# Memory scores moved to the next pair's second turn, and two multiplications of the output norm given out later

## The chip, the cores and the metric

The kernel runs on one core of one Trainium2 chip. Its metric is the time of one execution in microseconds (us), as the device measures it. Below, TensorE (PE in the profile) does the matmuls and the transposes, VectorE (DVE) and ScalarE (ACT) the elementwise work and the reductions, GpSimd (POOL) masks and some products, and SyncE (SP) issues most of the DMAs. PEld in the profile is the loading of a matmul's stationary operand.

## The reference

One layer of a hybrid decoder over 4096 prompt tokens, with a small batch of 64 sampled tokens beside it, all in float32 with a model width of 1024:

```python
h = _rmsnorm(x, g_pre)
z = h @ w_in                       # one projection for all three groups
...
out_a = jax.nn.silu(cg) * cb * conv              # gated short convolution, 256 channels
o_b = _window_prompt(q, k, v, sink_g)            # window of 128, 8 heads of 64, sinks
out_b = jax.nn.silu(ag) * o_b
o_c = _mem_attend(mq, mem_k, mem_v)              # 4 heads into 256 memory tokens
out_c = jax.nn.silu(mg) * o_c
y = jnp.concatenate([out_a, out_b, out_c], axis=-1) @ w_out
return x + _rmsnorm(y, g_post), ...
```

Two pieces matter here. The memory attention's softmax is `exp(s - max)` over 256 keys, divided by its sum. And the output norm is `y * rsqrt(mean(y * y) + eps) * g_post`, added to `x`.

## The kernel before

**Stages.** The input projection fills the first part of the span: its last matmuls of line 368 end at 935.9 us. Then attention and output projection run together. The 4096 tokens are 16 chunks of 256, and each chunk has two halves of 128 queries, numbered h (chunk h // 2, half h % 2). The output projection takes the first six blocks of 128 tokens plainly (class `Block`, lines 1579 to 1661), and the other 26 blocks as 13 pairs (class `Pair`, line 1663 on), c = 3 to 15. A pair multiplies two blocks with both column halves of `w_out` by a scheme of sums and differences that needs fewer products. Each operand is split into a rounded high part and a low part (`lows`, line 1675: an ACT cast, then a DVE subtraction), and three matmuls (high by high, low by high, high by low) make one step of 128 in depth.

**Turns.** `Pair.run` (line 1730) issues 30 such steps, called turns here, of three matmuls of 128x512 each. In order: turns 0 and 1 (T3) and 2 and 3 (T4) start the accumulators c12 and c21; 4 and 5, then 6 and 7, add the row sums `pr`; 8 to 11 add `pw0` into c12; 12 and 13 add `pw1` into c21; 14 and 15 start c11 with the diagonal sum `pd`; 16 and 17 end c21; 18 and 19 add the differences `pc`; 20 to 23 end c11; 24 and 25 start c22; 26 to 29 end it. Before the matmuls of a turn, the functions registered for it are called, in the order of registration.

**Attention by turns.** Three functions serve a half h. `first_half(h)` (line 1885) transposes the memory probabilities of half h-1 (`xt`, line 1366), multiplies the window scores of h (`ws`, line 1331), multiplies both probabilities of h-1 with the values (lines 1388, 1394, 1059) and issues the window softmax. `memory_half(h)` (line 1906) multiplies the memory scores of h (`xs`, line 1353), and issues their maxima (`xmx`, line 1169), the negatives of these (`xnm`, line 1170), the exponentials (line 1178, ACT), the reciprocals of the sums (line 1184, DVE) and the factors on the probabilities (line 1190, POOL). `second_half(h)` (line 1912) transposes the window probabilities (`wt`, line 1376), copies them (line 1305, ACT), masks them on POOL in two selections each (`wpv`, line 1310, and `wpt`, line 1313), and loads keys and queries of half h+2. In a pair c from 3 on, half 2c+3 has them at turns 12, 16 and 19, and half 2c+4 at turns 24, 27 and 32; turn 32 is turn 2 of the next pair. Below, halves 2c+3 are the odd ones and 2c+4 the even ones.

**Order.** In pairs 3 to 12 TensorE runs in the order in which the program is written (`manual_schedule`). On the other engines a planner places each instruction when the kernel is compiled: of those that it takes to be ready by its own costs, the one written first. `keep_in_program_order(ins)` adds one edge: `ins` comes behind the instruction written just before it on its engine. On the chip each engine then follows its own order.

**Buffers.** The scores `xs`, the transposes `xt` and the products `wo` share one place of two PSUM banks. Four accumulators a pair share two more banks in turn. A high and low part takes one of four slots left in the pool of the weights. The queries have two slots, so those of half h+2 wait for the readers of half h.

**Ends of a pair.** A finished quarter is copied or added into `y`, squared on ACT with a sum (`square`, line 1748), and multiplied by the norm's weights `gpost` on DVE (line 1760 in `squared`, line 1770 in `scaled`, which for the first block of a pair is on POOL). `Block.finish` (line 1655) scales the row and adds `x` (line 1658).

Of the kernel before, what the change touches and what calls it, by code (L numbers as in the profile page):

```python
# [8 lines left out]
F32 = mybir.dt.float32  # L9
# [3 lines left out]
ALU = mybir.AluOpType  # L13
AX = mybir.AxisListType

P = 128
# [11 lines left out]
NCH = 4096 // CT  # L28
EPS = 1e-6
SCALE = 0.125  # L30
# [22 lines left out]
def hybrid_layer(ctx: ExitStack, tc: tile.TileContext, a: dict):  # L53
    nc = tc.nc
    TE, V, S, G, DMA = nc.tensor, nc.vector, nc.scalar, nc.gpsimd, nc.sync
# [14 lines left out]
    diag = const.tile([P, 2 * HW], F32, name="mix_s")  # L70
# [835 lines left out]
    last = NBLK - 1  # L906
# [161 lines left out]
    class Chunk:  # L1068
# [94 lines left out]

            return *(self.cross_unit(2 * j + hh, pts[hh]) for hh in range(2)), both

        def cross_maximum(self, h, s):
            c, nb = self.c, CT // P
            mx, nm = (tiny.tile([P, 4], F32, tag=n, name=f"x{n}{c}_{h}") for n in ("mx", "nm"))
            V.tensor_reduce(mx[:, :nb], s, axis=AX.X, op=ALU.max)
            V.tensor_scalar(nm[:, :nb], mx[:, :nb], -SCALE, None, op0=ALU.mult)  # L1170
            return nm

        def cross_exps(self, h, s, nm, p=None):
# [173 lines left out]
        def memory_scores(self, i):  # L1347
            c = self.c
            x = two_banks("x", f"xs{c}_{i}").rearrange("p a (h k) -> p a h k", h=2)
            for h in range(4):  # L1350
                q = self.q[i][:, h]
                for part in range(2):
                    TE.matmul(x[:, h // 2, h % 2], q, third["mk"][:, part, h, :], start=part == 0, stop=part == 1)  # L1353
            nms = [self.cross_maximum(2 * i + j, x[:, j]) for j in range(2)]
            self.xp = work([P, 2, 2, CT], "p", f"xp{c}_{i}")
            self.xps = [self.cross_exps(2 * i + j, x[:, j], nms[j], self.xp[:, j]) for j in range(2)]
            for j in range(2):
                self.cross_shares(2 * i + j, self.xps[j])
# [304 lines left out]
    class Pair:  # L1663
# [50 lines left out]

        def diagonal_sum(self):
            self.diagonal = self.parts("pd")[:, :, 0:2]
            self.sums_of(sums["sum"].tile([P, 512], F32, tag="sum", name=f"diag{self.c}"), self.diagonal, (self.mix(slice(2, 4), 0), self.mix(slice(0, 2), 1), ALU.add))()

        def column_differences(self):
            t = self.parts("pc")  # L1720
# [9 lines left out]
        def run(self, starts, sample=lambda: None):  # L1730
            c, last = self.c, self.c == NCH - 1
            t, at = third["wt"], [0]
            b11, b22 = [wo[2 + k][0] for k in range(2)], [wo[k][1] for k in range(2)]
            y = self.y = [work([P, D], "yn", f"yn{c}_{n}") for n in range(2)]
# [13 lines left out]
            def square(n, p, src, junk, pinned=False):  # L1748
                x = S.activation(junk, src, AF.Square, scale=float(D) ** -0.5, accum_out=st[n][:, p : p + 1])
                if pinned:  # L1750
                    tc.keep_in_program_order(x)
# [3 lines left out]
                S.copy(y[n][:, cs], acc)  # L1755

            def squared(n, p):
                cs = (left_, right_)[p]
                square(n, p, y[n][:, cs], s4, True)
                V.tensor_tensor(y[n][:, cs], y[n][:, cs], gpost[:, cs], op=ALU.mult)  # L1760

            def added(n, p, acc):
# [33 lines left out]
            done(1, 0, c21)  # L1796
            product(c11, self.down[1], t["T7"], False)
            squared(1, 0)
            product(c11, self.w[0], plain(0, range(4, 8)), False)
            added(0, 0, c11)  # L1800
            if not last:
                c22 = psum("z", f"y{c}_c22")
                between.append(lambda: (scaled(0, 0, True), ends(0)))
                product(c22, self.down[0], t["T6"], True)
                product(c22, self.w[1], plain(1, range(4, 8)), False)
                added(1, 1, c22)
                while behind:
                    behind.pop(0)()
                scaled(1, 1)
                ends(1)  # L1810
                return
# [59 lines left out]
    PLAIN_PAIRS = 3  # L1871
# [58 lines left out]

    first_at = {2: 4, 3: 20, 4: 34, 5: 48, 6: 62, 7: 76, 8: 89}
    turn_of = lambda odd, even: {h: start_of((h - 3) // 2) + (odd if h % 2 else even) for h in range(9, 2 * NCH + 1)}
    memory_at = {h: n + (7 if h == 2 else 3 if h == 8 else 3) for h, n in first_at.items()} | turn_of(16, 27)
    second_at = {h: n + (12 if h == 2 else 9 if h == 8 else 8) for h, n in first_at.items()} | turn_of(19, 32)
    first_at |= turn_of(12, 24)

# [3 lines left out]
    def at(n, fn):  # L1940
        what.setdefault(n, []).append(fn)
# [17 lines left out]
    for c, p in pairs.items():  # L1959
        e = start_of(c)  # L1960
        at(e - 10, p.plain_parts)
        at(e - 3, p.row_sums)
        if c == NCH - 2:
            at(e + 27, lambda: left.pop(0)(True))
        at(e + 4, lambda p=p: p.window_parts(0))
        at(e + 5, lambda: pending.pop()() if pending else None)
        at(e + 6, lambda: left.pop(0)(True) if left else None)
        at(e + (5 if c == NCH - 1 else 7), lambda p=p: p.window_parts(1))
        at(e + (7 if c == NCH - 1 else 9), p.diagonal_sum)
        at(e + (8 if c == NCH - 1 else 11), p.column_differences)  # L1970
        at(e + (9 if c == NCH - 1 else 11), lambda p=p: p.differences(True) if p.c == NCH - 1 else between.append(lambda: p.differences(True)))
        at(start_of(c - 1) + 6, p.load)
        if c == NCH - 1:
            at(e + 4, finish_block)
# [146 lines left out]
```

## Time and profile before

| what | value |
|---|---|
| three executions | 1522.27, 1523.91 and 1524.03 us; median 1523.91 |
| the profiled execution | 1528.73 us, of which the span from first to last instruction is 1527.0 us |
| busy, of the span | PE 99%, PEld 91%, DVE 79%, ACT 55%, POOL 26% |
| granted TensorE clock, mean | 0.998 |
| starts of pairs 3, 4 and 5 | 1049.87, 1086.51 and 1121.98 us |
| start of pair 15, and the end | 1476.55 and 1527.0 us |

A row of the timeline has the start, the time from the first to the last of the merged instructions, the engine, the line, the operation, what is written and read, the shape and the count; in brackets stands the idle time of the engine before it and what ended that. The profile counts a matmul as busy to its modelled end, which lies beyond the start of the next one, so a short wait of TensorE can lie inside its busy time. What a wait costs is read from the starts: a turn of three matmuls begins 0.69 us after the one before it when nothing holds it.

### The profile page before, as it was taken

How to read it: one execution, taken by the hardware profiler on the slowest of the kernel's cores; microseconds unless marked ns; L12 is line 12 of the kernel's file. 1: busy time of each engine (PE TensorE's matmuls, PEld its weight loads, DVE VectorE, ACT ScalarE, POOL GpSimd, SP SyncE). 2: the span in 40 equal slices, each digit the busy share in tenths (PEclk: the TensorE clock that was granted, in tenths of full speed). 3: DMA queues.
4: the chain of work that ended last, by engine and by line, in shares of the span. 5: the costliest groups of instructions: out<-in, count | busy, mean ns of one | idle time of the engine just before them, and what ended most of it. 6: DMA issues, size and time to landing. Idle time of an engine off the chain costs nothing.

```text
span 1527.0 us, 30947 instructions
## 1 busy us (share of the span) xinstructions
PE 1507.6 (99%) x11497; PEld 1384.4 (91%) x11497; DVE 1199.3 (79%) x2089; ACT 843.5 (55%) x2066; POOL 398.5 (26%) x576
## 2 busy tenths in 40 slices
PE   9999999999999999999999999999999999999997
PEld 8999999999999999999999999777888788888875
DVE  5779887899988777897677768777877788878874
ACT  5776665566322222354455536666666666666652
POOL 0223322211400000000111311234445544455641
PEclk9999999999999999999999999999999999999999
DMA  9989999978855333478687698988765555666552
GB/s 258 168 250 221 289 290 259 265 243 303 209 183 182 118 121 126 161 235 295 222 261 232 213 305 254 282 241 235 201 169 160 156 164 161 175 171 170 153 196 75
DMA packets 217322, 319.71 MB, mean 209 GB/s; under 512 B 37397, under 2 KB 143381, under 8 KB 217141
## 3 DMA queue, kind: packets, MB, share of 16 engines
q1 hardware_dynamic: 196837, 273.54, 60.8%
q0 software_dynamic: 19616, 43.15, 10.5%
q8 instruction: 91, 1.49, 0.4%
q10 hardware_dynamic: 720, 1.05, 0.2%
q14 instruction: 58, 0.48, 0.1%
HBM read 208.50 MB, written 110.15 MB: 209 GB/s over the span
## 4 chain that ended last, share of the span: by engine, by line
PE 75%; DMA 11%; DVE 6%; issue 4%; POOL 2%; ACT 1%; SPq 1%; DVEq 0%; ACTq 0%; POOLq 0%
PE c L368 39%; PE y_c L1746 16%; PE y L1637 3%; PE ws L1331 3%; DMA nat<-in_x_p 2%; DMA md<-th 2%; PE wo L1394 2%; PE wo L1059 2%; PE xs L1353 2%; PE xt L1366 2%; PE wt L1376 2%; PE wo L1388 2%; DMA place<-in_xt 1%; DMA wr_3A<-in_w_in 1%; DMA hd_B<-place 1%
## 5 line engine op out<-in xcount | busy, mean ns | idle before, releaser
L375 DVE TENSOR_TENSOR z<-c,z 128x520 f32<-128x520 f32 (+1 forms) x308 | 194.6, 645 | 83.5 <-PE c L368 82.5
L1746 PE MATMUL y_c<-wo,pw 128*128 128x512 f32 (+1 forms) x636 | 158.9, 392 | 0.6 <-DVE yn L1784 0.6
L1287 ACT ACTIVATE sm<-sm,wnm 128x128 f32<-128x128 f32 x256 | 99.4, 389 | 72.0 <-DVE wnm L1281 72.0
L1746 PEld LDWEIGHTS y_c<-wo,pw 128*128 128x128 f32 x636 | 114.0, 188 | 27.8 <-issue 5.4
L1190 POOL TENSOR_SCALAR xp<-xp,xrd 128x256 f32<-128x256 f32 x128 | 71.8, 577 | 196.9 <-DVE xrd L1184 192.3
L1178 ACT ACTIVATE xp<-xs,xnm 128x256 f32<-128x256 f32 x128 | 59.0, 473 | 38.3 <-DVE xnm L1170 22.9
L737 POOL CAST wmask<-negs 128x256 uint8<-128x256 f32 x1 | 1.1, 1149 | 266.6 <-DMA negs<-in_wmask 266.6
L1637 PE MATMUL y<-wo,mh 128*128 128x512 f32 x192 | 64.5, 398 | 0.2 <-ACT y L1646 0.2
L1310 POOL TENSOR_SCALAR_AFFINE_SELECT wpv<-wpt 128x512 f32<-128x512 f32 x62 | 56.9, 939 | 8.7 <-ACT wpt L1305 8.4
L1313 POOL TENSOR_SCALAR_AFFINE_SELECT wpt<-wpt 128x512 f32<-128x512 f32 x64 | 46.3, 742 | 38.6 <-ACT wpt L1305 38.2
L1331 PE MATMUL ws<-kst,q 128*128 128x256 f32 (+1 forms) x480 | 55.7, 297 | 0.0
L1341 DVE COPY_PREDICATED sm<-wmask,ws 128x512 f32<-128x512 uint8 x60 | 40.5, 729 | 19.0 <-ACT sm L1340 19.0
L276 ACT ACTIVATE nat<-nat 104x1024 f32<-104x1024 f32 x40 | 42.3, 1058 | 23.6 <-DMA nat<-in_x_p 23.5
L1658 DVE SCALAR_TENSOR_TENSOR xr<-yn,yst,xr 128x1024 f32<-128x1024 f32 (+2 forms) x35 | 51.3, 1470 | 2.9 <-POOL yst L1653 2.8
L407 ACT CAST zh<-z 128x520 fp32r<-128x520 f32 x56 | 33.3, 624 | 34.6 <-DVE z L375 31.9
L377 ACT COPY z<-c 128x520 f32<-128x520 f32 (+1 forms) x44 | 24.4, 554 | 50.5 <-PE c L368 47.2
L1331 PEld LDWEIGHTS ws<-kst,q 128*128 128x128 f32 (+1 forms) x480 | 46.4, 187 | 4.1
L1287 ACT ACTIVATION_READ_ACCUMULATOR sm<-sm,wnm 128x1 f32 x256 | 47.9, 187 | 0.0
L1295 DVE TENSOR_TENSOR sm<-sm,wrd 128x512 f32<-128x512 f32 x64 | 44.5, 696 | 1.1
L1746 PE MATMUL y_c<-wo,pc 128*128 128x512 f32 (+1 forms) x162 | 45.2, 400 | 0.0
L164 POOL DMA_DIRECT2D md<-th x48 | 26.3, 549 | 71.3 <-DVE th L425 61.0
L1637 PEld LDWEIGHTS y<-wo,mh 128*128 128x128 f32 x192 | 36.1, 188 | 8.9 <-issue 1.0
(1037 smaller groups left out, 5556.9 us busy)
## 6 DMA issues: line engine op xcount, KB each, us to landing
q<-qd SPq DMA_DIRECT2D x168, 128.0 KB
xr<-in_x_p SPq DMA_DIRECT2D x32, 512.0 KB
nat<-in_x_p SPq DMA_DIRECT2D x39, 416.0 KB
o_yp<-xr SPq DMA_DIRECT2D x31, 512.0 KB
kst<-qd SPq DMA_DIRECT2D x112, 128.0 KB
md<-th POOLq DMA_DIRECT2D x48, 260.0 KB, 7.2
qd<-zh SPq DMA_DIRECT2D x48, 260.0 KB
qd<-z SPq DMA_DIRECT2D x48, 260.0 KB
```

Source lines behind the costliest of these rows:

```text
L368: TE.matmul(bank[:, :HW], l, r, start=first and i == 0, stop=last and i == 3 * KH - 1)
L375: add = lambda dst, other: V.tensor_tensor(dst, c, other, op=ALU.add)
L1178: S.activation(p[:, i, :], s[:, i, :], AF.Exp, bias=nm[:, i : i + 1], scale=SCALE, accum_out=den[:, i : i + 1])
L1190: G.tensor_scalar(p[:, i, :], p[:, i, :], self.rds[h][:, i : i + 1], 0.5, op0=ALU.mult, op1=ALU.mult)
L1287: S.activation(sm[:, hh, :], sm[:, hh, :], AF.Exp, bias=nm[:, hh : hh + 1], scale=SCALE, accum_out=den[:, hh : hh + 1])
L1295: V.tensor_tensor(sm, sm, rd.unsqueeze(2).to_broadcast([P, 4, P]), op=ALU.mult)
L1310: G.affine_select(pv.rearrange("p (h q) -> p h q", h=4), p3, pattern=[[0, 4], [-1, P]], compare_op=ALU.is_gt, fill=0.0, base=0, channel_mu ...
L1313: G.affine_select(p3, p3, pattern=[[0, 4], [1, P]], compare_op=ALU.is_ge, fill=0.0, base=0, channel_multiplier=-1)
L1331: TE.matmul(out(kvh, col, bank), q(kvh, col, bank)[r], k(kvh, part)[r], start=first, stop=True, skip_group_check=not first, **place)
L1637: TE.matmul(acc, self.hl[l][:, k], wo[k][p][:, r], start=k + i == 0, stop=k + i == KT + 1)
L1658: x = V.scalar_tensor_tensor(self.xr[:m, cs], yn[:m, cs], st[:m, 3:4], self.xr[:m, cs], op0=ALU.mult, op1=ALU.add)
L1746: TE.matmul(acc, a[:, l, k], w[:, r, cs], start=first, stop=k == len(ws) - 1 and i == 2, skip_group_check=not new)
```

## The change

Four things are moved or bound.

- `cross_maximum` can bind the negative behind the instruction written before it on DVE, and `memory_scores` asks for that.
- The memory scores of the even halves are issued at turn 32 in place of turn 27, so at turn 2 of the next pair, behind the transposes and loads of `second_half` of the same half. That holds for halves 10 to 30, eleven in all.
- The parts of the window's outputs, `pw0` and `pw1`, are issued at turns 1 and 2 in place of 4 and 7 (4 and 5 in the last pair). Both of their instructions stay bound behind what is written before them on ACT and DVE.
- In `squared` the multiplication by `gpost` becomes a function of its own, `gained`. That of the first block's right half, written after turn 13 so far, is written after turn 19; that of the second block's left half, after turn 19 so far, is written after turn 25 (in the last pair directly behind the other). In the first pair the low part of the diagonal sum is bound behind what is written before it on DVE.

No instruction is added or taken out.

```diff
-        def cross_maximum(self, h, s):
+        def cross_maximum(self, h, s, pinned=False):
             c, nb = self.c, CT // P
             mx, nm = (tiny.tile([P, 4], F32, tag=n, name=f"x{n}{c}_{h}") for n in ("mx", "nm"))
             V.tensor_reduce(mx[:, :nb], s, axis=AX.X, op=ALU.max)
-            V.tensor_scalar(nm[:, :nb], mx[:, :nb], -SCALE, None, op0=ALU.mult)
+            negated = V.tensor_scalar(nm[:, :nb], mx[:, :nb], -SCALE, None, op0=ALU.mult)
+            if pinned:
+                tc.keep_in_program_order(negated)
             return nm
...
-            nms = [self.cross_maximum(2 * i + j, x[:, j]) for j in range(2)]
+            nms = [self.cross_maximum(2 * i + j, x[:, j], True) for j in range(2)]
...
         def diagonal_sum(self):
             self.diagonal = self.parts("pd")[:, :, 0:2]
-            self.sums_of(sums["sum"].tile([P, 512], F32, tag="sum", name=f"diag{self.c}"), self.diagonal, (self.mix(slice(2, 4), 0), self.mix(slice(0, 2), 1), ALU.add))()
+            x = self.sums_of(sums["sum"].tile([P, 512], F32, tag="sum", name=f"diag{self.c}"), self.diagonal, (self.mix(slice(2, 4), 0), self.mix(slice(0, 2), 1), ALU.add))()
+            if self.c == PLAIN_PAIRS:
+                tc.keep_in_program_order(x)
...
             def squared(n, p):
+                square(n, p, y[n][:, (left_, right_)[p]], s4, True)
+
+            def gained(n, p):
                 cs = (left_, right_)[p]
-                square(n, p, y[n][:, cs], s4, True)
                 V.tensor_tensor(y[n][:, cs], y[n][:, cs], gpost[:, cs], op=ALU.mult)
...
             product(c11, self.down[1], t["T7"], False)
             squared(1, 0)
+            gained(0, 1)
+            if last:
+                gained(1, 0)
             product(c11, self.w[0], plain(0, range(4, 8)), False)
             added(0, 0, c11)
             if not last:
                 c22 = psum("z", f"y{c}_c22")
                 between.append(lambda: (scaled(0, 0, True), ends(0)))
                 product(c22, self.down[0], t["T6"], True)
+                gained(1, 0)
                 product(c22, self.w[1], plain(1, range(4, 8)), False)
...
-    memory_at = {h: n + (7 if h == 2 else 3 if h == 8 else 3) for h, n in first_at.items()} | turn_of(16, 27)
+    memory_at = {h: n + (7 if h == 2 else 3 if h == 8 else 3) for h, n in first_at.items()} | turn_of(16, 32)
...
-        at(e + 4, lambda p=p: p.window_parts(0))
+        at(e + 1, lambda p=p: p.window_parts(0))
         at(e + 5, lambda: pending.pop()() if pending else None)
         at(e + 6, lambda: left.pop(0)(True) if left else None)
-        at(e + (5 if c == NCH - 1 else 7), lambda p=p: p.window_parts(1))
+        at(e + 2, lambda p=p: p.window_parts(1))
```

## The prediction

> **What bounds the kernel now.** I read the page's engine table first, then the windows of the third and of an ordinary pair, then the table of waits over the pair stage, then the timeline of each engine around the waits that stood out.
>
> ```profile
> PE 1507.6 (99%) x11497; PEld 1384.4 (91%) x11497; DVE 1199.3 (79%) x2089; ACT 843.5 (55%) x2066; POOL 398.5 (26%) x576
> ```
>
> TensorE bounds the whole span, and no work of it is removed. So the change can only take away or add moments in which TensorE stands still. The next view is the windows of pair 3 (1049.87 to 1086.51) and of a later pair: columns are the stretch, its length, then PE, PEld, DVE, ACT, POOL and SP busy, and the granted clock last but two.
>
> ```profile
> 1049.87:1086.51 36.64, 35.89 (x237) 28.80 (x236) 26.68 (x63) 23.96 (x82) 15.63 (x23) 1.00 0.82 207
> 1192.95:1228.45 35.50, 35.50 (x237) 28.69 (x236) 28.48 (x65) 24.02 (x82) 17.43 (x23) 1.00 0.60 168
> ```
>
> The clock is 1.00 in both. The later pair shows PE busy throughout, but this is by modelled ends; the loads fill only 28.69 of 35.50. The table of waits of the loads, over 1049 to 1527 (total us, times, longest), finds what lies hidden; its largest row that this change touches:
>
> ```profile
> PEld wo L1388 <- POOL wpt L1313: 4.1, 11, 0.4
> ```
>
> Eleven times, once a pair, the products with the window probabilities (line 1388) wait for POOL's last selection. In the timeline (start, length, engine, line, operation, what is written and read, shape, count), first at turn 12 and then at turn 24:
>
> ```profile
> 1204.94 0.43 PE L1388 MATMUL wo<-wpv,vt 64*64 64x256 f32 x2
> ...
> 1205.54 0.65 PE L1394 MATMUL wo<-wpv,vt 128*64 128x256 f32 x4
> ```
>
> ```profile
> 1220.21 0.43 PE L1388 MATMUL wo<-wpv,vt 64*64 64x256 f32 x2
> ...
> 1221.36 0.65 PE L1394 MATMUL wo<-wpv,vt 128*64 128x256 f32 x4
> ```
>
> At turn 12 the group of line 1388 takes 0.60 (1204.94 to 1205.54); at turn 24 it takes 1.15 (1220.21 to 1221.36): 0.55 lost. The chain behind it, on DVE, ACT and POOL:
>
> ```profile
> 1212.05 0.66 DVE L1169 TENSOR_REDUCE xmx<-xs 128x2 f32<-128x512 f32 x1
> 1212.63 0.68 DVE L1295 TENSOR_TENSOR sm<-sm,wrd 128x512 f32<-128x512 f32 x1
> 1213.23 0.69 DVE L1760 TENSOR_TENSOR yn<-yn,gpost 128x512 f32<-128x512 f32 x1
> 1213.83 0.16 DVE L1170 TENSOR_SCALAR xnm<-xmx 128x2 f32<-128x2 f32 x1
> 1213.90 0.68 DVE L1169 TENSOR_REDUCE xmx<-xs 128x2 f32<-128x512 f32 x1
> ```
>
> ```profile
> 1214.68 0.47 ACT L1178 ACTIVATE xp<-xs,xnm 128x256 f32<-128x256 f32 x1 [1.25 <-DVE xmx L1169]
> ```
>
> ```profile
> 1216.08 1.85 POOL L1190 TENSOR_SCALAR xp<-xp,xrd 128x256 f32<-128x256 f32 x4 [5.83 <-DVE xrd L1184]
> 1217.88 1.68 POOL L1310 TENSOR_SCALAR_AFFINE_SELECT wpv<-wpt 128x512 f32<-128x512 f32 x2
> 1219.51 1.22 POOL L1313 TENSOR_SCALAR_AFFINE_SELECT wpt<-wpt 128x512 f32<-128x512 f32 x2
> ```
>
> POOL works without a gap from 1216.08 to 1220.73. It was idle for 5.83 before, until a reciprocal. That came from exponentials, for which ACT had stood idle 1.25 until the second maximum ended at 1214.58. And DVE put a multiplication by `gpost` (line 1760, 0.60 from start to start) between the first maximum and its negative.
>
> **The change part by part.**
>
> *Multiplications given out later (odd halves).* Line 1760 is now written after turn 19, behind the maxima of turn 16. The second maximum and all that follows start 0.60 earlier. The loss is only 0.55, so it would be gone,. But ready by then, line 1760 can still slip in between the second maximum and its negative; the first exponentials then start as early, the second 0.60 later than they could, and POOL has two of its four factors to do meanwhile (0.93, half of 1.85), so I lose 0.1 of it. The gain lies between 0.4 and 0.55; I take 0.45. Eleven pairs: 11 x 0.45 = 4.95 less, at most 6.05. The multiplication itself moves into slack: its result is read only by `finish` in the next pair. In the last pair nothing moves but one multiplication, beside idle time; nothing.
>
> *Pins on the negatives.* Each reads the maximum written just before it. The edge holds an order that data holds already: the row at 1213.83 comes behind 1212.05 in any case, and nothing forbids the planner to put others between. Zero, from both sides, for the waits; what the planner then orders differently is in the range.
>
> *The third pair.* Here the low part of `pw0` and of the diagonal go ahead of what TensorE needs:
>
> ```profile
> 1054.42 0.69 DVE L1781 TENSOR_TENSOR s<-s,y_c 128x512 f32<-128x512 f32 x1 [1.57 <-PE y_c L1746]
> 1055.03 1.07 DVE L1679 TENSOR_TENSOR pw<-mix,pw 128x512 fp32r<-128x512 f32 x1
> 1056.02 0.85 DVE L1679 TENSOR_TENSOR pd<-diag,pd 128x256 fp32r<-128x256 f32 x1
> 1056.80 0.67 DVE L1784 TENSOR_TENSOR yn<-s,y_c 128x512 f32<-128x512 f32 x1
> ```
>
> ```profile
> 1054.15 2.88 PE L1746 MATMUL y_c<-wo,pr 128*128 128x512 f32 x12
> 1057.61 3.00 PE L1746 MATMUL y_c<-wo,pw 128*128 128x512 f32 x12 [0.58 <-DVE yn L1784]
> ```
>
> The same two groups of TensorE in the later pair:
>
> ```profile
> 1196.80 2.96 PE L1746 MATMUL y_c<-wo,pr 128*128 128x512 f32 x12
> 1199.59 2.94 PE L1746 MATMUL y_c<-wo,pw 128*128 128x512 f32 x12
> ```
>
> From the row sums to `pw0` it takes 3.46 in pair 3 and 2.79 in the later pair, so 0.67 is lost. With `pw0` at turn 1 its low part falls into DVE's idle 1.57 ahead of 1054.42, and the diagonal goes behind what it is written after. Gain 0 to 0.67; I take 0.6. This happens once.
>
> *Memory scores at turn 32 (even halves).* The eight matmuls of `xs` leave turn 27 and come at turn 2 of the next pair. TensorE's work is the same; DVE's and POOL's queue changes. DVE, in the order of the later pair, and the load of TensorE that waits for it:
>
> ```profile
> 1196.13 0.21 DVE L1652 TENSOR_SCALAR yst<-yst 128x1 f32<-128x1 f32 x1 [0.45 <-ACT s L1749]
> 1196.26 1.17 DVE L1770 TENSOR_TENSOR yn<-yn,gpost 128x512 f32<-128x512 f32 x1
> 1197.36 0.68 DVE L1781 TENSOR_TENSOR s<-s,y_c 128x512 f32<-128x512 f32 x1
> 1198.10 0.70 DVE L1679 TENSOR_TENSOR pw<-mix,pw 128x512 fp32r<-128x512 f32 x1
> ```
>
> ```profile
> 1198.09 1.23 PEld L1746 LDWEIGHTS y_c<-wo,pr 128*128 128x128 f32 x6 [0.18 <-DVE s L1781]
> ```
>
> The sum of line 1781 ends at 1198.04 and TensorE's second half of the row sums, which reads it, is loaded from 1198.09, after 0.18 of waiting: no slack. Before it now come the two maxima. When can they start? The moved `xs` stand behind these transposes, and as their time has left turn 27, they end about where the transposes end now, near 1195.4:
>
> ```profile
> 1194.32 1.03 PE L1376 MATMUL wt<-ident,sm 128*128 128x128 f32 x8
> ```
>
> From there DVE has the maxima (0.58 each, 1212.05 to the next start), the tiny row (0.13 to the next start), line 1770 and perhaps the low part of `pw0` (0.61 to the next start, an estimate from the 0.60 of its kind above). With line 1770 at 0.60 the sum starts at 1197.3 without the low part, 1197.9 with it, against 1197.36 now: 0 to 0.55 late. With line 1770 at the 1.17 that it takes today it would be 1.0 late at the worst. Its cost hangs on what POOL does beside it:
>
> ```profile
> L1770 DVE TENSOR_TENSOR yn<-yn,gpost x12: 682/1168/1174, 1089.8 to 1478.4; 128x512 f32<-128x512 f32 x12
> ```
>
> The columns are least, median and most in ns: 0.68 occurs. POOL's factors of the memory, beside it today, move behind this place, so I count with 0.68. I take the low part ahead of the sum in one pair of four, 0.15 a pair, 11 x 0.15 = 1.65 more, and keep 0 to 0.6 (6.6).
>
> `pw1` goes to turn 2 with its cast and low part bound behind what is written before them; it is due only at turn 12. Loads of queries for half h+2 wait for the later `xs`, and SP's other loads behind them, but the next reader comes 22 turns later, some 15 us. Both cost nothing, unless a queue is held; the bound is the second rival's.
>
> POOL of the even half (the factors, then behind them the selections and a difference), and the transposes on TensorE that read the factors:
>
> ```profile
> 1196.86 1.38 POOL L1190 TENSOR_SCALAR xp<-xp,xrd 128x256 f32<-128x256 f32 x2
> ```
>
> ```profile
> 1199.18 2.21 POOL L1310 TENSOR_SCALAR_AFFINE_SELECT wpv<-wpt 128x512 f32<-128x512 f32 x2
> 1201.34 1.67 POOL L1313 TENSOR_SCALAR_AFFINE_SELECT wpt<-wpt 128x512 f32<-128x512 f32 x2
> 1202.98 1.46 POOL L1693 TENSOR_TENSOR yn<-mix 128x512 f32<-128x512 f32 x1
> ```
>
> ```profile
> 1202.37 1.03 PE L1366 MATMUL xt<-ident,xp 128*128 128x128 f32 x8
> ```
>
> Selections (3.88 together) now go ahead of the factors (2 x 1.38 = 2.76). TensorE needs the factors at turn 12, from 1202.37, the last of them half of the group later, so about 1202.8, or 1202.3 with TensorE 0.45 earlier. The 6.6 of work can begin when the transposes `wt` are done, at 1195.4, and end at 1202.0; if the difference of 1.46 goes ahead of the last factors, at 1203.5. I take 1202.3, no wait, and keep 0 to 1.2 a pair for the range.
>
> Sum: -4.95 - 0.6 + 1.65 = -3.9. The profiled execution (1528.73, span 1527.0) becomes 1524.8; it stands 4.8 above the median of 1523.91, so for the median: 1520.0. A change under 0.2% (3.05 us) can't be told from none here.
>
> **A rule of the skill against the trace.** Line 1760, by its line:
>
> ```profile
> L1760 DVE TENSOR_TENSOR yn<-yn,gpost x26: 683/756/1074, 1071.2 to 1499.3; 128x512 f32<-128x512 f32 x26
> ```
>
> The rows of line 1770 (0.68 at least, 1.17 mostly) and of line 1760 (0.68 to 1.07) show that these multiplications take longer at some places than at others; the place at 1196.26 has POOL's factors beside it. The Trainium skill, page "SBUF — State Buffer", section "Who interferes with whom", says that a DVE instruction with two SBUF inputs contends with a GpSimd instruction that reads SBUF, and that the loser stands still for all of the other; the trace agrees at line 1770. By that rule the multiplication, moved to turn 19 and later, would take time from POOL's chain between 1216 and 1220.7: by the rule the sum is 1525.0, the third rival's; without it, 1520.0.
>
> **The rivals.**
>
> 1. *The even half's DVE queue gives the gain back.* For it speaks that line 1781 has no slack now; against it, the 0.49 by which line 1770 should be shorter. The low part of `pw0` goes ahead of the sum in every pair, 0.55 a pair in place of 0.15: 11 x 0.4 = 4.4 more than forecast, 1524.4, no change.
>
> 2. *POOL's factors come too late for turn 12 (the other side).* For it: 3.88 of selections now go ahead of them, and a difference of 1.46 may. Against: POOL had 5.83 of idle in the odd half, and its queue isn't full. It decides from an end of the factors after 1202.3 on; at 1203.2 TensorE waits 0.9 a pair, 11 x 0.9 = 9.9 more than my sum has, and 1.65 goes out since line 1781 has then no wait behind an earlier one: 1520.0 + 9.9 - 1.65 = 1528.3. At an end of 1202.5 it is 0.2 a pair and the kernel is as fast as forecast.
>
> 3. *The moved multiplication slows POOL.* The two factors at 1196.86, beside line 1770, take 1.38, where half of the four at 1216.08 take 0.93: 0.45 lost. In the odd chain that takes the whole 0.45 back: 1520.0 + 4.95 = 1525.0, and some of it is saved where line 1760 falls in a selection: 1523 to 1525. No change.
>
> 4. *The place is filled anyway.* The planner puts something else of 0.6 between the first maximum and its negative, so the odd wait stays. Only pair 3's 0.6 is left: 1523.91 - 0.6 = 1523.3. For it speaks that DVE has a window factor (1212.63) in that place already; against it, that I find nothing else of that length written near it.
>
> **How the numbers follow.** The forecast has 0.48: both ends of its chain are in the trace, and the loss it takes away is the largest of the stage. Its own range is 1517.2 (6.05 + 0.67 gained, nothing lost) to 1521.5 (4.4 gained by the odd halves at 0.4 each, nothing in pair 3, 2.0 lost at line 1781). Rival 1 has 0.18, rival 3 0.06, rival 4 0.06: these make 0.30 for no change. Rival 2 has 0.22, since its end of the factors is my least certain number. The range reaches from the best of the forecast, 1517, to just above rival 2, 1528.5; what lies outside is a worse POOL queue or a gain in the even half that I don't see.
>
> **What would show it.** Right: the wait of line 1388 for the selection gone or below 0.1 a time, its group at turn 24 near 0.6; pairs of 35.0 to 35.3 in place of 35.5; pair 3 near 35.7; line 1770 near 0.68 in most pairs. Wrong by rival 1: a PE wait for line 1781 of 0.4 and more. By rival 2: a wait of the transposes `xt` for line 1190 at turn 12. By rival 3: factors of the odd half longer than 1.85 beside line 1760. By rival 4: still 1.2 between first maximum and negative. The wait of PE at turn 0 or 2 for `wt` would be a cause that I have not counted.

## The result: slower by 0.7%

The changed kernel takes 1533.91 us (median of 7 runs, 1531.54 to 1543.91), the kernel before 1523.91 (7 runs, 1521.59 to 1527.91). The ratio is 1.007, with a 95% interval of 1.005 to 1.009. The forecast was 1520.0, its range 1517.0 to 1528.5.

The profiled execution took 1543.91 us (span 1542.0), 10 above the median. Of the 15.2 by which it is longer than that of before, 3.6 lie ahead of pair 3, which starts at 1053.50 in place of 1049.87; over the profiled executions shown here this start varies between 1041.4 and 1053.5, so no reading is taken from it. From the start of pair 3 to that of pair 15 it is 438.2 in place of 426.7: 11.5 more, all of it in the pairs. The medians differ by 10.0.

The page of after, its engine table:

```profile
span 1542.0 us, 30982 instructions
PE 1511.8 (98%) x11497; PEld 1386.7 (90%) x11497; DVE 1196.5 (78%) x2089; ACT 842.4 (55%) x2066; POOL 392.2 (25%) x576
```

The work is the same, and each engine is as busy as before to within 1 or 2%, POOL 6 us less. The span grew by waiting. The windows of pair 3 and of an ordinary pair (stretch, length, then PE, PEld, DVE, ACT, POOL and SP busy, clock last but two):

```profile
1053.50:1088.19 34.69, 34.41 (x230) 27.68 (x228) 26.08 (x60) 23.43 (x82) 15.49 (x23) 1.00 0.85 205
1198.24:1234.94 36.70, 35.61 (x237) 28.65 (x236) 28.33 (x65) 23.99 (x83) 16.80 (x23) 1.00 0.56 162
```

An ordinary pair is 1.2 longer than before (36.70 against 35.50), at the same clock of 1.00, and now PE's own row has the hole: 35.61 busy of 36.70. The loads' waits over the pair stage (total us, times, longest):

```profile
PEld y_c L1750 <- DVE s L1787: 11.3, 11, 1.1
...
PEld xt L1368 <- POOL xp L1192: 9.0, 22, 0.5
```

The wait of line 1388 (now 1390) for the selection `wpt` at turn 24 is gone from the head of this table. Two others took its place: the row sums wait for the sum of line 1781 (now 1787), once a pair, and the transposes `xt` for POOL's factors, twice a pair. Both stand in the even half, on TensorE (start, length, engine, line, idle before and what ended it):

```profile
1203.04 1.53 PE L1750 MATMUL y_c<-wo,pr 128*128 128x512 f32 x6
1205.25 1.66 PE L1750 MATMUL y_c<-wo,pr 128*128 128x512 f32 x6 [0.67 <-DVE s L1787]
1206.74 2.90 PE L1750 MATMUL y_c<-wo,pw 128*128 128x512 f32 x12
1209.48 0.60 PE L1368 MATMUL xt<-ident,xp 128*128 128x128 f32 x4
1210.37 1.00 PE L1368 MATMUL xt<-ident,xp 128*128 128x128 f32 x4 [0.29 <-POOL xp L1192]
1211.13 1.85 PE L1333 MATMUL ws<-kst,q 128*128 128x256 f32 x16
```

The row sums take 3.70 from their start to that of `pw0` (1203.04 to 1206.74), 0.91 more than the 2.79 of before; the transposes take 1.65 (1209.48 to 1211.13), where four and four of them took 0.79 before, 0.86 more. At turn 24 the products take 1.55, 0.52 less than in the same pair of before:

```profile
1228.16 0.43 PE L1390 MATMUL wo<-wpv,vt 64*64 64x256 f32 x2
...
1229.71 1.04 PE L1059 MATMUL wo<-xp,mkv 128*64 128x128 f32 x16
```

Together that is 1.25, close to the 1.20 of the pair.

What DVE and POOL did meanwhile:

```profile
1201.33 0.98 DVE L1776 TENSOR_TENSOR yn<-yn,gpost 128x512 f32<-128x512 f32 x1
1202.24 0.68 DVE L1681 TENSOR_TENSOR pw<-mix,pw 128x512 fp32r<-128x512 f32 x1
1202.84 1.28 DVE L1169 TENSOR_REDUCE xmx<-xs 128x2 f32<-128x512 f32 x2
1204.04 0.57 DVE L1170 TENSOR_SCALAR xnm<-xmx 128x2 f32<-128x2 f32 x1
1204.52 0.67 DVE L1787 TENSOR_TENSOR s<-s,y_c 128x512 f32<-128x512 f32 x1
...
1205.84 0.68 DVE L1790 TENSOR_TENSOR yn<-s,y_c 128x512 f32<-128x512 f32 x1
1206.44 1.28 DVE L1660 SCALAR_TENSOR_TENSOR xr<-yn,yst,xr 128x1024 f32<-128x1024 f32 x1
1207.65 0.15 DVE L1186 RECIPROCAL xrd<-xden 128x2 f32<-128x2 f32 x1
```

```profile
1202.72 1.28 POOL L1312 TENSOR_SCALAR_AFFINE_SELECT wpv<-wpt 128x512 f32<-128x512 f32 x2
1203.96 1.22 POOL L1315 TENSOR_SCALAR_AFFINE_SELECT wpt<-wpt 128x512 f32<-128x512 f32 x2
1206.02 1.97 POOL L1192 TENSOR_SCALAR xp<-xp,xrd 128x256 f32<-128x256 f32 x2 [0.85 <-DVE xrd L1186]
1207.96 1.73 POOL L1695 TENSOR_TENSOR yn<-mix 128x512 f32<-128x512 f32 x1
1209.67 1.10 POOL L1192 TENSOR_SCALAR xp<-xp,xrd 128x256 f32<-128x256 f32 x2
```

Ahead of the sum at 1204.52 stand the low part of `pw0` (0.60 to the next start), two maxima, and a negative of 128x2 elements that takes 0.57, where the same instruction took 0.16 before. POOL's selections were done by 1205.18, and then POOL waited 0.85 for a reciprocal. The second reciprocal (1207.65) stood behind the end of a block (line 1660), and POOL took a difference of 1.73 between its two pairs of factors. So there are four suspects: the low part, the negative, the end of the block, and the loss of whatever the odd gain should have given.

### The profile page after: what moved, and what is told of

Same layout as the page of the kernel before. It is cut to its first block, busy times and chain, and to the rows that moved or that the text cites. A ratio compares the mean times of both kernels' runs of the same rounds, so it can differ in the third digit from the quotient of the medians.

```text
span 1542.0 us, 30982 instructions
## 1 busy us (share of the span) xinstructions
PE 1511.8 (98%) x11497; PEld 1386.7 (90%) x11497; DVE 1196.5 (78%) x2089; ACT 842.4 (55%) x2066; POOL 392.2 (25%) x576
## 5 line engine op out<-in xcount | busy, mean ns | idle before, releaser
L1192 POOL TENSOR_SCALAR xp<-xp,xrd 128x256 f32<-128x256 f32 x128 | 76.9, 616 | 146.2 <-DVE xrd L1186 141.7
L1660 DVE SCALAR_TENSOR_TENSOR xr<-yn,yst,xr 128x1024 f32<-128x1024 f32 (+2 forms) x35 | 48.4, 1388 | 3.4 <-POOL yst L1655 3.3
L1315 POOL TENSOR_SCALAR_AFFINE_SELECT wpt<-wpt 128x512 f32<-128x512 f32 x64 | 41.0, 659 | 38.1 <-ACT wpt L1307 37.7
L1312 POOL TENSOR_SCALAR_AFFINE_SELECT wpv<-wpt 128x512 f32<-128x512 f32 x62 | 46.6, 773 | 9.0 <-ACT wpt L1307 8.8
L1369 ACT COPY xp<-xt 128x1024 f32<-128x1024 f32 x30 | 30.4, 1014 | 33.4 <-PE xt L1368 31.5
L1750 PE MATMUL y_c<-wo,pr 128*128 128x512 f32 x156 | 41.3, 401 | 6.6 <-DVE s L1787 6.6
L1753 ACT ACTIVATE s<-yn 128x512 f32<-128x512 f32 (+1 forms) x53 | 33.3, 629 | 24.0 <-DVE yn L1770 21.7
```

The source lines that it names most:

```text
L1192: G.tensor_scalar(p[:, i, :], p[:, i, :], self.rds[h][:, i : i + 1], 0.5, op0=ALU.mult, op1=ALU.mult)
L1312: G.affine_select(pv.rearrange("p (h q) -> p h q", h=4), p3, pattern=[[0, 4], [-1, P]], compare_op=ALU.is_gt, fill=0.0, base=0, channel_mu ...
L1315: G.affine_select(p3, p3, pattern=[[0, 4], [1, P]], compare_op=ALU.is_ge, fill=0.0, base=0, channel_multiplier=-1)
L1660: x = V.scalar_tensor_tensor(self.xr[:m, cs], yn[:m, cs], st[:m, 3:4], self.xr[:m, cs], op0=ALU.mult, op1=ALU.add)
L1750: TE.matmul(acc, a[:, l, k], w[:, r, cs], start=first, stop=k == len(ws) - 1 and i == 2, skip_group_check=not new)
```

## The experiments

The columns are differences of starts on TensorE, as medians of pairs 4 to 12: the pair; the products at turn 24 (the odd wait, 1.51 unheld); the last six matmuls ahead of the row sums, which hold a wait for the copy of c12 (1.39 unheld); the row sums (2.78 in the kernel before); the transposes of turn 12 (0.79 unheld). Ratios are to the kernel before on the same chip, with 95% intervals.

| kernel | ratio | pair | turn 24 | before row sums | row sums | turn 12 |
|---|---|---|---|---|---|---|
| before | 1 | 35.49 | 2.06 | 1.47 | 2.78 | 0.79 |
| changed | 1.007 (1.005 to 1.009) | 36.66 | 1.56 | 1.39 | 3.68 | 1.63 |
| e1_weights | 1.0006 (0.999 to 1.0021) | 35.43 | 1.52 | 1.77 | 2.93 | 0.79 |
| e2_scores | 1.013 (1.0108 to 1.0151) | 37.22 | 2.02 | 1.39 | 4.54 | 0.79 |
| e3_scores_back | 1.0045 (1.003 to 1.006) | 35.97 | 1.51 | 2.29 | 3.02 | 0.79 |
| e4_parts_back | 1.0126 (1.0105 to 1.0146) | 37.19 | 1.51 | 1.39 | 5.02 | 0.79 |
| e5_square_later | 0.9984 (0.9968 to 0.9999) | 35.41 | 1.56 | 1.47 | 3.21 | 0.79 |
| e6_square_only | 0.9991 (0.9973 to 1.0009) | 35.48 | 2.07 | 1.47 | 2.78 | 0.79 |
| e7_low_later | 1.0002 (0.9986 to 1.0019) | 35.59 | 1.53 | 1.39 | 3.36 | 0.79 |
| e8_negatives | 1.004 (1.0024 to 1.0056) | 36.29 | 1.53 | 1.39 | 3.24 | 1.67 |
| e9_finish_later | 0.9996 (0.9986 to 1.0005) | 35.30 | 1.72 | 1.47 | 2.89 | 0.79 |
| e10_finish_only | 1.0014 (1.0005 to 1.0022) | 35.70 | 2.19 | 1.47 | 2.77 | 0.79 |
| e11_both | 1.0051 (1.0034 to 1.0068) | 36.13 | 1.52 | 1.39 | 2.77 | 1.92 |
| e12_best | 0.998 (0.9972 to 0.9989) | 35.28 | 1.72 | 1.47 | 2.86 | 0.79 |
| e13_end_later | 0.9942 (0.9922 to 0.9962) | 34.97 | 1.51 | 1.39 | 2.78 | 0.79 |
| e14_end_only | 1.0017 (1.0003 to 1.0032) | 35.82 | 1.51 | 1.39 | 3.74 | 0.79 |
| e15_four | 0.9935 (0.9913 to 0.9957) | 34.96 | 1.51 | 1.39 | 2.78 | 0.79 |

The pins on the negatives had no run of their own: without them the planner writes the same order on every engine.

### The parts alone: e1 to e4

The edit of e1, on the kernel before (the two calls of the new function stand where the change has them):

```diff
             def squared(n, p):
+                square(n, p, y[n][:, (left_, right_)[p]], s4, True)
+
+            def gained(n, p):
                 cs = (left_, right_)[p]
-                square(n, p, y[n][:, cs], s4, True)
                 V.tensor_tensor(y[n][:, cs], y[n][:, cs], gpost[:, cs], op=ALU.mult)
```

> The kernel before with one part of the change alone: the two multiplications by the norm's weights are given out later, everything else stays. Theory A (the parts add up: this one takes the wait at turn 24 away, the moved scores cost more than that): the products of turn 24 take 1.55 in place of 2.06, pairs 35.0 in place of 35.5, 1523.9 - 11 x 0.5 = 1518.4 us. Rival C (the moved multiplication slows GpSimd's chain): the products stay near 2.0 and the time near 1523.9.

The odd wait went as expected, from 2.06 to 1.52, but the pair lost only 0.06, and the time did not move. The gain went to the next turns. The loads of TensorE in the pair that starts at 1191.96:

```profile
1196.08 1.22 PEld L1746 LDWEIGHTS y_c<-wo,pr 128*128 128x128 f32 x6 [0.54 <-ACT s L1781]
1197.51 1.21 PEld L1746 LDWEIGHTS y_c<-wo,pr 128*128 128x128 f32 x6 [0.21 <-DVE s L1783]
1198.96 1.21 PEld L1746 LDWEIGHTS y_c<-wo,pw 128*128 128x128 f32 x6 [0.23 <-ACT pd L1676]
```

The first waits for ACT's copy of c12 (its line is 1781 here, 1779 in the kernel before), the second for the sum. So the odd wait lay in the shadow of a longer chain, which begins ahead of it, at the window scores of turn 24, and runs over the softmax, the maxima and the exponentials to that copy:

```profile
1192.87 0.69 DVE L1295 TENSOR_TENSOR sm<-sm,wrd 128x512 f32<-128x512 f32 x1
```

```profile
1193.00 0.47 ACT L1178 ACTIVATE xp<-xs,xnm 128x256 f32<-128x256 f32 x1 [1.56 <-DVE xnm L1170]
...
1194.82 0.64 ACT L1749 ACTIVATE s<-yn 128x512 f32<-128x512 f32 x1
...
1195.43 0.59 ACT L1781 COPY s<-y_c 128x512 f32<-128x512 f32 x1
```

The copy ends at 1196.02 and the row sums are loaded from 1196.08. TensorE comes earlier and the chain does not.

e2 is the kernel before with one number changed, and e3 the changed kernel with it changed back:

```diff
-    memory_at = {...} | turn_of(16, 27)
+    memory_at = {...} | turn_of(16, 32)
```

> The kernel before with only the memory scores of the even halves moved to turn 32; window parts at turns 4 and 7, multiplications by the weights where they were, no pins. Theory A: the two maxima stand ahead of the sum that the row sums wait for and the factors come late for the transposes at turn 12: pairs longer by 0.4 to 1.2, 1528 to 1537 us. Rival B (the harm is done by the window parts at turns 1 and 2, which put a low part ahead of the sum): no change, 1523 to 1525 us, row sums 2.8 long.

> The changed kernel with the memory scores of the even halves back at turn 27; all else as changed. Theory A: the gains stay and the losses go: pairs 35.0, pair 3 about 36.1, row sums 2.8, transposes of turn 12 0.79: 1517.5 to 1518.5 us, faster than before. Rival B: the window parts at turns 1 and 2 still stand ahead of the sum: row sums near 3.4 and 1523 us or more.

Both were misses. The moved scores alone cost 1.73 a pair, more than the 0.4 to 1.2 expected, and in another place: turn 8, where `pw0` begins. On ACT its cast now stands behind the exponentials (1196.61, after the last of them at 1196.16), on DVE its low part and the difference behind it come late, and TensorE waits:

```profile
1196.61 1.14 ACT L1676 CAST pw<-mix 128x512 fp32r<-128x512 f32 x2
```

```profile
1198.78 2.98 PE L1746 MATMUL y_c<-wo,pw 128*128 128x512 f32 x12 [1.62 <-DVE yn L1784]
```

In e3 the early parts have the opposite fault: the cast of `pw0` goes ahead of the copy of c12 on ACT, and the six matmuls before the row sums take 2.29.

```profile
1194.68 1.23 PEld L1750 LDWEIGHTS y_c<-wo,pr 128*128 128x128 f32 x6 [1.08 <-ACT s L1785]
```

e4 takes the early parts out of the changed kernel:

```diff
-        at(e + 1, lambda p=p: p.window_parts(0))
+        at(e + 4, lambda p=p: p.window_parts(0))
...
-        at(e + 2, lambda p=p: p.window_parts(1))
+        at(e + (5 if c == NCH - 1 else 7), lambda p=p: p.window_parts(1))
```

> The changed kernel with the window parts back at turns 4 and 7. Theory A: the low part of pw0 (0.60) no longer stands ahead of the sum, so the row sums take 3.1 in place of 3.7, and the factors come 0.6 earlier, the transposes of turn 12 take 1.0 to 1.6: 1521 to 1528 us. Rival B: both losses vanish, 1518 us.

It is slower again, for the reason of e2, and `pw0` is even later. It is e2 with the multiplications moved and the pins set; beside e2 the odd wait is 0.51 shorter (2.02 and 1.51), the row sums are 0.48 longer (4.54 and 5.02), and the pair is the same (37.22 and 37.19). So neither theory held: the moved scores and the early parts each cost when alone (1.73, and 35.97 less 35.43 = 0.54 on top of the moved multiplications), and together less than the scores alone. They belong together, because with the scores at turn 2 ACT's exponentials (1204.70 in the pair shown of the changed kernel) come behind the early cast (1201.08) and the copy (1201.58).

### Shortening the chain in the kernel before: e5, e6, e9, e10, e12

e5 adds to e1 that the last square of a pair, and what follows it, is written in the next pair behind the copy; e6 is this edit alone. In the cut below, `late[0]` is the square, bound behind the copy.

```diff
             S.copy(s3, c12)
+            late = carried.pop() if carried else []
+            if late:
+                late[0]()
...
-                scaled(1, 1)
-                ends(1)
+                carried.append((lambda: square(1, 1, y[1][:, right_], s4, True), rest))
```

> The kernel of the run with the later multiplications alone, and besides, the last square of a pair and what follows it (factor, multiplication, end of the block) written in the next pair behind the copy of c12 into s3, so that ACT does the copy first. Theory A2 (the odd wait lay in the shadow of a longer chain, from the window scores of turn 24 over softmax, maxima and exponentials to that copy; the copy is what TensorE then waits for at turn 4): the copy comes 0.6 earlier, the second six matmuls before the row sums take 1.4 in place of 1.75, pairs 35.0 to 35.1 and 1518 to 1519 us. Rival D (another instruction of the same chain, the sum on DVE, is as late): pairs stay at 35.4, 1523 us.

> The kernel before with the last square of a pair behind the copy of c12, and nothing else. Theory A2: the copy had 0.1 to 0.2 of slack there, so the copy's part of a pair shrinks by less than 0.1, and the wait at turn 24 stays (products 2.0 to 2.06): pairs 35.4 to 35.5, 1522.5 to 1524 us. If the copy alone were what costs, 1518 us.

The copy came earlier and no longer holds (1.47), but the sum of DVE does, to the same end: the row sums take 3.21 and the pair is 35.41, as long as in e1, where 35.0 to 35.1 was expected. That is rival D. e6 does nothing, as expected.

e9 adds to e1 that the end of a pair's first block, 1.84 us on DVE that stood in the middle of the window softmax, is written at the end of the pair; e10 is this alone; e12 is e9 with the pin on the diagonal's low part in pair 3.

```diff
-            finish_block(True)
+            if i or not PLAIN_PAIRS + 2 <= self.c:
+                finish_block(True)
...
+                if c < NCH - 2:
+                    left.pop(0)(True)
                 scaled(1, 1)
```

> The kernel before with the two multiplications given out later, and besides, the end of a pair's first block (scale and add of x, 1.84 us on DVE) written at the end of the pair in place of turn 24, where it stands between the window exponentials and their sums. Theory A3 (the odd wait lay in the shadow of a chain from the window scores of turn 24 over DVE's softmax, the maxima and ACT's exponentials to the copy and the sum that turns 4 and 6 need; this end of a block is its one link that could be elsewhere): the chain is 1.1 us shorter, nothing takes the odd wait's place: products of turn 24 1.5, six matmuls before the row sums 1.4 to 1.5, row sums 2.75 to 2.85, pairs 35.0, 5 to 6 us under the kernel before. Rival D2 (the chain is held elsewhere too): pairs stay at 35.4, within 2 us of the kernel before.

> The kernel before with that end of the first block at the end of the pair, and nothing else. Theory A3: the chain gets slack, but the odd wait at turn 24 stays (products 2.0 to 2.06): pairs 35.4 to 35.5, within 2 us of the kernel before. If the chain alone set the pair, 5 us less.

> The kernel of the run with the end of the first block later and the multiplications later, and besides the diagonal's low part of the third pair bound behind what is written before it. Theory A3: pairs 35.0, the third pair's row sums 2.75 in place of 3.46: 6 to 7 us under the kernel before (0.4%). Rival D2: within 2 us of it.

Half a hit. In e9 the row sums are nearly free (2.89), but 0.2 of the odd wait is back (1.72) and the pair is 35.30, not 35.0; e10 is slower by 0.14%, with a longer odd wait (2.19). Why the odd half's POOL chain ends later there by 0.1 to 0.2 was not followed up. e12 is faster than both kernels (0.998). Its third pair has row sums of 2.72 in place of 3.46, and is 35.33 in place of the 36.10 of e9.

### The even half of the changed kernel: e7, e8, e11, e13, e14, e15

e7 writes the low part of `pw0` behind the sum and binds it there (`self.low` below; its cast stays at turn 1), e8 makes the negatives on ACT, e11 does both:

```diff
             V.tensor_tensor(s4, s3, c21, op=ALU.add)
+            self.low()
...
-            negated = V.tensor_scalar(nm[:, :nb], mx[:, :nb], -SCALE, None, op0=ALU.mult)
-            if pinned:
-                tc.keep_in_program_order(negated)
+            if pinned:
+                S.mul(nm[:, :nb], mx[:, :nb], -SCALE)
+            else:
+                V.tensor_scalar(nm[:, :nb], mx[:, :nb], -SCALE, None, op0=ALU.mult)
```

> The changed kernel with one instruction moved: the low part of pw0 is written behind the sum that the row sums wait for. Theory A2: that part is 0.60 of the 0.93 lost there: row sums 3.1 in place of 3.7; the reciprocals come earlier too, the transposes of turn 12 take 0.8 to 1.1 in place of 1.63: pairs 35.4 to 35.8, 1521 to 1525 us. Rival E (the maxima and the negative alone make the sum late): row sums stay above 3.5 and the time above 1530 us.

> The changed kernel with the negatives of the memory maxima made on ACT in place of DVE. Theory A2: the first negative stood 0.57 in place of 0.16 beside GpSimd's selection, and 0.41 of the row sums' loss is that: row sums 3.3 in place of 3.7, transposes of turn 12 1.2 to 1.6: pairs 35.9 to 36.3, 1525 to 1530 us. Rival F (the long negative only fills time in which the sum had to wait anyway): no change, 1533 to 1534 us.

> The changed kernel with both: the low part of pw0 behind the sum, and the negatives on ACT. Theory A3: the two are the whole of what the row sums lost (0.93 = 0.60 less what the one run left, and 0.41): row sums 2.8 to 3.0, transposes of turn 12 0.8, pairs 35.0 to 35.3, 2 to 6 us under the kernel before. If something else holds the sum, row sums stay at 3.3 and the kernel is as fast as the kernel before.

Without DVE's negative the row sums go from 3.68 to 3.24, near the 3.3 of theory A2. Without the low part ahead of the sum they go to 3.36, about half of the gain expected (3.1). Without both they are at 2.77, unheld: the two together are enough to take away the whole loss there. e7 freed the transposes too, because its other order on DVE put the second reciprocal ahead of the block's end. In e8 and e11 it stayed behind, and e11 lost at turn 12 what it had won (1.92). DVE and POOL in e11:

```profile
1198.74 1.45 DVE L1661 SCALAR_TENSOR_TENSOR xr<-yn,yst,xr 128x1024 f32<-128x1024 f32 x1
1200.11 0.15 DVE L1187 RECIPROCAL xrd<-xden 128x2 f32<-128x2 f32 x1
```

```profile
1200.51 1.72 POOL L1696 TENSOR_TENSOR yn<-mix 128x512 f32<-128x512 f32 x1
1202.21 1.09 POOL L1193 TENSOR_SCALAR xp<-xp,xrd 128x256 f32<-128x256 f32 x2
```

So the last three runs write that end of a block at turn 9 in place of 6: e13 on e11, e14 on the changed kernel alone, e15 as e13 with the low part moved from pair 4 on only.

```diff
-        at(e + 6, lambda: left.pop(0)(True) if left else None)
...
+        at(e + 9, lambda: left.pop(0)(True) if left else None)
```

> The kernel of the run with the low part later and the negatives on ACT, and besides, the end of a pair's second block (1.45 us on DVE) written at turn 9 in place of 6, so that the second reciprocal of the memory stands ahead of it. Theory A4 (the factors were late for turn 12 because that reciprocal stood behind the end of the block, and GpSimd took a difference of 1.72 meanwhile): the factors run without a gap, the transposes of turn 12 take 0.79 in place of 1.93, pairs 35.0 to 35.1, 4 to 6 us under the kernel before. Rival G (the factors are late because the exponentials are): the transposes stay above 1.4 and the kernel is slower than before.

> The changed kernel with only that end of a block at turn 9. Theory A4: the transposes of turn 12 take 0.8 to 1.0 in place of 1.63, the row sums stay at 3.7: pairs 35.8 to 36.0, 1526 to 1527 us where the kernel before has 1523.9. Rival G: no change, pairs 36.65.

> The run with all three edits, with the low part of pw0 moved in pairs 4 to 15 only, since in the third pair moving it made the row sums longer. Theory A4: 1 us under that run, third pair's row sums 2.7 to 3.0, 5 to 7 us under the kernel before, which would be as fast as the best kernel so far or faster.

Theory A4 held in all three. In e14 the transposes are free and the other columns moved by 0.06 at most: the pair is 0.84 shorter (36.66 to 35.82), just what turn 12 had lost. POOL still idles 0.85 there ahead of its first factor, so it is the second reciprocal, and the difference that came in between, that cost. In e13 no turn of the even half is longer than unheld:

```profile
1153.68 0.15 DVE L1187 RECIPROCAL xrd<-xden 128x2 f32<-128x2 f32 x1
1153.76 0.66 DVE L1797 TENSOR_TENSOR yn<-s,y_c 128x512 f32<-128x512 f32 x1
1154.36 0.17 DVE L1187 RECIPROCAL xrd<-xden 128x2 f32<-128x2 f32 x1
```

```profile
1154.24 2.27 POOL L1193 TENSOR_SCALAR xp<-xp,xrd 128x256 f32<-128x256 f32 x4
```

```profile
1146.89:1181.86 34.97, 34.97 (x237) 28.61 (x236) 27.60 (x61) 24.34 (x87) 15.98 (x23) 1.00 0.59 170
```

POOL does the four factors without a gap, and the pair is 34.97, busy throughout. e15 is the fastest of all: 1511.72 us where the kernel before took 1520.50 on that chip, 0.9935 with an interval of 0.9913 to 0.9957. Both gained more than expected: e13 6.9 us where 4 to 6 were, e15 8.8 where 5 to 7 were. So the change, with these three edits, is faster than the kernel before; the best run without the moved scores is e12 (0.998). The three edits without the moved scores were not run.

## Why the prediction was wrong

Two terms of the sum failed, the 4.95 gained and the 1.65 lost, and with them one wait that was put at nothing.

**The odd wait: right in mechanism and size, but the gain did not stay.** The multiplication left its place. Between the first maximum and its negative now stands 0.60 of a window factor, where 1.20 stood before:

```profile
1220.02 0.66 DVE L1169 TENSOR_REDUCE xmx<-xs 128x2 f32<-128x512 f32 x1
1220.60 0.68 DVE L1297 TENSOR_TENSOR sm<-sm,wrd 128x512 f32<-128x512 f32 x1
1221.20 0.16 DVE L1170 TENSOR_SCALAR xnm<-xmx 128x2 f32<-128x2 f32 x1
```

The products of turn 24 fell by 0.50 in the changed kernel, 0.54 in e1, where 0.45 was forecast. The first step that failed is "Eleven pairs: 11 x 0.45 = 4.95 less". e1 shows that the pair gains 0.06 of it: the rest turns into waits for the copy of c12 and for the sum. The step from e2 to e4 shows the same with the scores moved. The changed kernel shows it too, by accident: in pair 4 the products of turn 24 still take 1.88, and in pair 5, right behind, TensorE comes that much later and waits 0.34 for the sum, where it waits 0.67 in the pair shown above (1205.25). The row sums of pair 5 take 3.37.

```profile
1118.18 0.43 PE L1390 MATMUL wo<-wpv,vt 64*64 64x256 f32 x2
...
1120.06 1.04 PE L1059 MATMUL wo<-xp,mkv 128*64 128x128 f32 x16
...
1131.91 1.66 PE L1750 MATMUL y_c<-wo,pr 128*128 128x512 f32 x6 [0.34 <-DVE s L1787]
```

So part of the loss at the sum, below, is this gain come back. How much in all is not shown, as the changed kernel without the later multiplications was not run. e13, with a shorter chain to the sum, keeps the gain: its pair is 0.52 shorter than before. The prediction looked for what is late next at the sum alone, and charged it to the moved scores. The copy on ACT, which in the kernel before ends at 1196.57 (1195.98 and 0.59) with the row sums loaded from 1196.63, was not looked at.

**The pins: right,** zero.

**The third pair: about right.** 0.6 forecast; the row sums went from 3.46 to 3.02, 0.44. The pin without the early `pw0` gives 0.74 (2.72 in e4 and e12), so the early `pw0` cost 0.3 there. With the negatives on ACT it costs nothing there (2.73 in e8).

**The sum on DVE: right place, wrong size.** The second step that failed is the term of 0.15 a pair, bounded by 0.6; it measured 0.90. "I take the low part ahead of the sum in one pair of four" was a guess: it stands there in all eleven pairs, 4 to 14, as rival 1 had it, and putting it behind the sum was worth 0.32 (3.68 to 3.36). The negative of 128x2, priced at nothing, took 0.57 in place of 0.16, and taking it off DVE was worth 0.44. Line 1770 (now 1776) was put at 0.68 and took 0.98 in the pair shown, and 0.98 or 0.99 in ten of the eleven pairs.

**The factors on POOL: forecast as no wait, measured 0.84 a pair.** Rival 2 had the place and the price (0.9) and half of the cause. The selections were not in the way: they ended at 1205.18, and POOL then idled 0.85. The factors waited for their reciprocals, the second of them behind the end of a block on DVE, and the difference of 1.73 came in between, as that rival had it. The third step that failed is "The 6.6 of work can begin when the transposes `wt` are done": the factors also need the exponentials and DVE's reciprocals, whose start the prediction never placed.

**Rival 3** did not come: in e1 the products of turn 24 are at 1.52, so the moved multiplication did not hold POOL's chain. In the changed kernel's odd half the two do not meet: the multiplication (line 1766, 1221.87 and 0.68) ends at 1222.55, and the four factors start at 1223.54 and take 1.84, as before (1.85). **Rival 4** did not come either: the place holds 0.60 in place of 1.20.

**The chances.** The rivals were treated as one or the other, and rival 2 took 1.65 out of its price because the sum would have no wait beside it. Rivals 1 and 2 came together: their two waits add to 1.74 a pair, 19 us over eleven pairs, and the range went only to rival 2 alone. They stand at different turns, and each can be there without the other: e14 has the wait for the sum alone, e11 the wait for the factors alone.

**The sum.** In an ordinary pair 0.90 and 0.84 more, 0.50 less at turn 24 and 0.08 less ahead of the row sums (1.47 to 1.39) make 1.16, of 1.17 measured. By the starts, pairs 4 to 13 are together 11.4 longer; pair 3 is 1.95 shorter, 0.95 of it since its last scores went to pair 4, and pair 14 2.07 longer, 0.95 of it by the scores that it received. That is the 11.5 by which the pairs are longer.

## What to carry to other kernels

A wait that is removed is worth the slack of the next thing that TensorE needs, not its own length; before pricing it, follow every operand of the following turns back on its own engine, and look for a chain that begins ahead of the wait. When a step moves, place its last consumer too: here it was a reciprocal of 0.15 us behind a block's end that cost 0.84 a pair. Two rivals that act at different turns can both come, so their prices add in the range.

## What the hardware showed that was not expected

In these traces a DVE instruction on 128x2 elements lasts up to as long as a GpSimd instruction beside it. In the changed kernel the first negative of an even half lasts 0.57, three and a half times its usual 0.16. The negatives by line (least, median, most in ns):

```profile
L1170 DVE TENSOR_SCALAR xnm<-xmx x64: 132/160/572, 823.5 to 1477.5; 128x2 f32<-128x2 f32 x64
```

Ten of the eleven even halves that moved have one of 0.57. The one at 1204.04 ends at 1204.61, as the first of two selections `wpt` does by half of its row (1203.96, 1.22 for both). In pair 12, which starts at 1381.53, it came later against POOL's work:

```profile
1387.31 0.20 DVE L1170 TENSOR_SCALAR xnm<-xmx 128x2 f32<-128x2 f32 x1
```

```profile
1386.27 1.22 POOL L1312 TENSOR_SCALAR_AFFINE_SELECT wpv<-wpt 128x512 f32<-128x512 f32 x2 [0.27 <-ACT wpt L1307]
1387.44 1.23 POOL L1315 TENSOR_SCALAR_AFFINE_SELECT wpt<-wpt 128x512 f32<-128x512 f32 x2
```

There it lasts 0.20 and ends at 1387.51, again with a selection (1386.27 and 1.22 is 1387.49), and this pair's row sums take 3.32 where those of its neighbours take 3.65 and 3.68, though its low part begins at the same place of the pair (3.99 after the start; 3.95 and 3.97 there). In e4 it starts elsewhere in the selection, lasts 0.50, and ends with it at 1197.1:

```profile
1196.63 0.50 DVE L1170 TENSOR_SCALAR xnm<-xmx 128x2 f32<-128x2 f32 x1
```

```profile
1195.89 1.22 POOL L1312 TENSOR_SCALAR_AFFINE_SELECT wpv<-wpt 128x512 f32<-128x512 f32 x2
```

In the traces of e2, e4 and e7 there are 35 negatives of 0.33 to 0.64, and each ends 0.02 to 0.03 after a selection. The Trainium skill, page "SBUF — State Buffer", section "Who interferes with whom", lists `tensor_scalar` among the operations that can take the ports shared with GpSimd, when their operands meet the conditions of a two-port mode, and says that whoever comes second stands still until the other's instruction is done; the trace agrees, since the negative came second and ended with the selection each time. The prediction had applied the rule to the large multiplications only. That it is the ports is not shown by itself; e8 shows that without the instruction on DVE the row sums are 0.44 shorter.
